# Norms between stages tile by tile, and act loads through GpSimd with one buffer less, in a 256-token model with expert retrieval

## The chip, the cores and the metric

One core of a Trainium2 chip runs the whole kernel. The time is that of one execution on the device in microseconds (us); lower is better. Engines: TensorE (PE) multiplies matrices, VectorE (DVE) and ScalarE (ACT) work on tiles of 128 partitions, GpSimd (POOL) and SyncE (SP) issue transfers (DMAs). Each engine runs its own list of instructions strictly in order and waits on semaphores for the others.

## The reference, cut to what matters

256 tokens of width 1024 pass through two blocks. The first block (attention, cross attention, feed-forward) ends in a norm. The second has two layers, each a mixer (an even and an odd kind) and an expert stage `peer`, with modulated norms ahead of both:

```python
x = _rmsnorm(x + (silu(gate) * up) @ w_down, final_norm)      # end of the first block
for l in range(2):
    h = rmsnorm(x, norm_mix[l]) * (1 + sc1) + sh1
    x = x + g1 * (even_mix(h) if l % 2 == 0 else odd_mix(h))
    h = rmsnorm(x, norm_ffn[l]) * (1 + sc2) + sh2
    x = x + g2 * peer(h, w_q[l], sub_keys[l], u[l], v[l])
return rmsnorm(x, final_norm_2)

def peer(h, w_q, sub_keys, u, v):            # per token t
    q = h @ w_q                              # 8 heads, two halves of 128
    top 16 of 128 x 128 keys by the scores of q against sub_keys, per head
    gate = softmax(the 16 scores)
    act = gelu(u[chosen] . h)
    return sum over heads and chosen of gate * act * v[chosen]
```

Everything is float32, and `u` and `v` have 16384 rows of 1024 each.

## The kernel before

Values of float32 are split into a high and a low half, and a product is three products on TensorE (high by high, high by low, low by high). Activations stand as `hl` tiles, channels on the partitions and the 256 tokens along the free axis; the tokens are two tiles `t` of 128. A weight comes as 1 MB `w` by a DMA that SyncE issues (`load_w`; in the V loop L1635); `split_w` makes its halves 512 columns at a time, the high one `wh` on ScalarE (L302), the low one `wl` on VectorE (L303). The ring `w` has three buffers, `wh`/`wl` five pairs.

The order of the stages: first block to about 366 us, where `w_down` ends (`proj`, with `ev_down` as what is done with its results); even_mix to 447; peer 0 to 1270; odd_mix to 1400; peer 1 to the end. Between two stages x is normed: `part_sq` (ScalarE, L154) sums squares of half a token tile, `inv_rms` makes 1/rms by a chain of some nine 128x1 instructions on VectorE (L181 to L199), `diag` (L212) puts it on a diagonal, and `to_T` (L267) multiplies x by the diagonal on TensorE, which transposes and scales it at once, 16 products of 128x128; `split_psum` (L249 to L255) adds the modulation and splits the result, pair of k by pair of k, into `hl`. While this goes on `keep_warm` (L287) lets TensorE run 80 products that nobody reads.

In `peer`, head by head, `feat2` multiplies h by `w_q` (L373 with the high half of the weight against 512 columns, L370 with the low half); its accumulators are two PSUM banks each, out of four banks in all (`acc_banks`, `acc_tile`). Then the top-16 search and the one-hot matrices `G` (gates of all experts, built from `onehots` and `build`) run beside the U stage, 64 passes of `feat2` over `u` that write `act` to DRAM in 256 KB pieces. The V loop follows, 64 passes: load 1 MB of `v`, split it (four `wh`, four `wl`), take 256 KB of `act` and of `G` for the same experts, and add 24 products of 512 columns to four accumulators (`wide_mm`, L423). `gated(n)` makes the activations for pass n: the load of `act` (SyncE, L1580) into `ag`, product by the gate `G` into `wt` (VectorE, L1582), its high half (ScalarE, L1589), its low half by subtraction (VectorE, L1590). `ag` and `wt` come from the ring `k2` with five buffers (NK2), as most temporaries do. In peer 0's V loop the modulation of the next layer is computed too, with an ada weight of 512 KB per pass (`ada_tick`; L482 loads it on SyncE, L483 multiplies on VectorE).

The order on each engine isn't written out: a scheduler walks through the program with estimated durations and queues instructions as they become ready, so it fixes each engine's list at build time; `follow` and `behind` give it hints.

Of the kernel before, what the change touches and what calls it, by code (L numbers as in the profile page):

```python
# [19 lines left out]
P = 128  # L20
S = 256
# [8 lines left out]
WARM = 80, 80, 80, 80  # L30
# [45 lines left out]
def body(tc, A, out, dbg=None, stop=None):  # L76
# [73 lines left out]
    def accum_sq(dst, src, eng):  # L150
        n = src.shape[-1]
        if eng == "a":
            j = st.tile([P, D], mybir.dt.bfloat16, name="k2", bufs=NK2)
            nc.scalar.activation(j[:, :n], src, AF.Square, accum_out=dst)  # L154
# [135 lines left out]

    def load_w(dram, off, per, ada=True):
# [6 lines left out]
    def split_w(src, n):  # L298

        h = sp.tile([P, 512], F32R, name="wh")  # L300
        l = sp.tile([P, 512], F32R, name="wl")
        ada_p["act"] = nc.scalar.activation(h[:, :n], src, AF.Copy).ins.name  # L302
        i_ = nc.vector.tensor_sub(l[:, :n], src, h[:, :n].bitcast(F32))  # L303
        ada_p["after"] = i_.ins.name
        return h, l
# [51 lines left out]
    def feat2(hl, dram, off, evac):  # L357
# [4 lines left out]
        for q in range(4):  # L362
            wh, wl = split_w(w[:, q * 512:(q + 1) * 512], 512)
            to = acc[:, q // 2]
            for i in range(4):
                k = (q % 2) * 4 + i
                ws = slice(i * P, (i + 1) * P)

                def low():
                    nc.tensor.matmul(to[:, 0, :], wl[:, ws], part(hl, k, 0), start=False, stop=False)  # L370
                if k == 7:
                    low()
                nc.tensor.matmul(to.rearrange("p a s -> p (a s)"), wh[:, ws],  # L373
                                 hl[k // 2][:, k % 2].rearrange("p a s -> p (a s)"), start=k == 0, stop=k == 7)
                if k < 7:
                    low()
            tick()
        evac(acc)

    def proj(hl, kc, dram, off, n, evac, base=0, quiet=0, turn=None):  # L380
# [10 lines left out]
        for k in order:  # L391
            m = min(4, kc - k)
            w = load_w(dram, off + k * P * n, m * n, len(order) - order.index(k) > quiet)
            j = 0
            while j < m:

                final = k == order[-1]
                js = [j, j + 1] if final and j == m - 2 else [j]
                if final and turn:
                    js = [turn[i] for i in js]  # L400
                ws = [split_w(w[:, q * n:(q + 1) * n], n) for q in js]
                last = None
                for t in range(2):
                    sl = slice(t * P, (t + 1) * P)
                    for q, (wh, wl) in zip(js, ws):
                        h_, l_ = pick(base + k + q, sl)
                        i_ = mm3(ps[t][:, :n], h_, l_, wh[:, :n], wl[:, :n], k == order[0] and j == 0 and q == js[0],
                                 final and j + len(js) == m and q == js[-1], after=last)
                        last = i_.ins.name if len(js) == 2 else None
                    if final and j + len(js) == m:  # L410
                        evac(t, ps[t][:, :n])
                for _ in js:
                    tick()
                j += len(js)
# [552 lines left out]

    def ev_down(hf):
        hs = slice(hf * 512, (hf + 1) * 512)

        def f(t, ps):
# [3 lines left out]
            part_sq(ssf, xf, t, hf, "a")  # L975
        return f
    ada_p["rate"] = RD
    for hf in range(2):
        proj(pick_g, 22, A["w_down"], hf * FF * 512, 512, ev_down(hf), quiet=hf)
# [3 lines left out]


    r1_ = nrm.tile([P, 2], F32, name="r1_", bufs=1)
    r2_ = nrm.tile([P, 4], F32, name="r2_", bufs=1)
    by0 = []
    for t in range(2):
        a_, b_ = ssx[:, 2 * t:2 * t + 1], ssx[:, 2 * t + 1:2 * t + 2]
        e_, c_ = r2_[:, 2 * t:2 * t + 1], r2_[:, 2 * t + 1:2 * t + 2]  # L990
        nc.vector.tensor_scalar(e_, a_, b_, D * EPS, op0=OP.add, op1=OP.add)
        nc.vector.tensor_scalar(e_, e_, EPS, None, op0=OP.mult)
        inv_rms(c_, ssf[:, 2 * t:2 * t + 1], ssf[:, 2 * t + 1:2 * t + 2], e_)
        by0.append(diag(c_))
    for t in range(2):
        inv_rms(r1_[:, t:t + 1], ssx[:, 2 * t:2 * t + 1], ssx[:, 2 * t + 1:2 * t + 2])
    if stop in ("mix", "cross", "b1"):
        for t in range(2):
# [17 lines left out]
    def x_scales(ss):  # L1016

        r = nrm.tile([P, 2], F32, name="rx2")
        out_ = []
        for t in range(2):  # L1020
            inv_rms(r[:, t:t + 1], ss[:, 2 * t:2 * t + 1], ss[:, 2 * t + 1:2 * t + 2])
            out_.append(diag(r[:, t:t + 1]))
        return out_
# [810 lines left out]
```

## Time and profile before

| | us |
|---|---|
| median of 3 runs | 2221.74 |
| lowest and highest | 2216.76, 2221.75 |
| profiled execution | 2223.68 |
| its span in the trace | 2221.9 |
| TensorE busy | 2183.6 (98%) |
| VectorE busy | 1826.7 (82%) |
| ScalarE busy | 1326.6 (60%) |
| GpSimd busy | 21.2 (1%) |

Busy shares are means over the span. The chain of work that ended last lies for 84% on TensorE, for 7% on VectorE and for 6% on the loads of `act`. By stretches: 40 slices of the page show TensorE at 9 tenths or more everywhere but at the two ends, and the DMA engines between 1 and 9 tenths, highest in peer 0's V loop (about 940 to 1270 us).

### The profile page before, as it was taken

The page shows a single profiled execution, that of the slowest core. Times are in us where ns is not written, and L with a number is a line of the kernel's source. Part 1 is how long each engine was busy: PE and PEld are TensorE (multiplying, and loading weights), DVE is VectorE, ACT ScalarE, POOL GpSimd, SP SyncE. Part 2 cuts the span into 40 slices and gives each one's busy share as a digit, 9 for nine tenths or more (in the row PEclk, how much of TensorE's full clock was granted, in tenths as well). Part 3 has the DMA queues.
Part 4 walks back from the last instruction along what each step waited for, and adds up shares of the span by engine and source line. Part 5 has one row for each costly group of instructions (what it writes and reads, how often), then busy time and mean ns, then how long its engine had stood idle before and what let it go on. Part 6 is the DMA issues. An engine that isn't in the chain of part 4 may idle for free.

```text
span 2221.9 us, 36167 instructions
## 1 busy us (share of the span) xinstructions
PE 2183.6 (98%) x12792; PEld 1865.7 (84%) x12792; DVE 1826.7 (82%) x4379; ACT 1326.6 (60%) x2448; POOL 21.2 (1%) x28
## 2 busy tenths in 40 slices
PE   8999999999999999999999999999999999999998
PEld 7889998888888888878777787888888888888886
DVE  7778888689988887688888888899888876777776
ACT  7656555555666666555555566566666666555554
POOL 0000000000000000000000010000000000000000
PEclk9999999999999999999999999999999999999999
DMA  6246787445655555889999643456555557666663
GB/s 244 96 167 256 271 303 281 160 173 206 226 212 207 198 212 209 283 314 332 323 321 322 215 157 122 171 193 239 203 201 210 196 212 259 250 248 245 244 240 143
DMA packets 107286, 503.30 MB, mean 227 GB/s; under 512 B 12513, under 2 KB 13665, under 8 KB 61794
## 3 DMA queue, kind: packets, MB, share of 16 engines
q1 hardware_dynamic: 87954, 465.19, 58.4%
q10 hardware_dynamic: 18864, 33.72, 4.1%
q8 instruction: 100, 1.64, 0.3%
q0 software_dynamic: 288, 2.10, 0.2%
q14 instruction: 80, 0.66, 0.1%
HBM read 464.25 MB, written 36.70 MB: 225 GB/s over the span
## 4 chain that ended last, share of the span: by engine, by line
PE 84%; DVE 7%; DMA 6%; ACT 1%; issue 1%; SPq 0%; DVEq 0%; ACTq 0%
PE acc L373 24%; PE acc L423 22%; PE acc L370 12%; DMA k<-act 6%; PE acc L308 4%; PE acc L311 4%; PE acc L312 4%; DVE wl L303 3%; PE acc L320 3%; PE acc L321 3%; PE acc L319 3%; PE mm L1547 1%; PE mm L1548 1%; DVE G L483 1%; PE pt L267 1%
## 5 line engine op out<-in xcount | busy, mean ns | idle before, releaser
L302 ACT ACTIVATE wh<-w 128x512 fp32r<-128x512 f32 (+1 forms) x1408 | 879.6, 630 | 652.6 <-PE acc L423 247.5
L303 DVE TENSOR_TENSOR wl<-w,wh 128x512 fp32r<-128x512 f32 (+1 forms) x1408 | 951.9, 689 | 205.7 <-ACT wh L302 198.2
L373 PE MATMUL acc<-q,wh 128*128 128x512 f32 x2240 | 797.3, 402 | 0.0
L423 PE MATMUL acc<-wh,q 128*128 128x512 f32 x1984 | 611.0, 390 | 0.0
L370 PE MATMUL acc<-q,wl 128*128 128x256 f32 x2240 | 584.3, 281 | 1.0 <-DVE wl L303 1.0
L373 PEld LDWEIGHTS acc<-q,wh 128*128 128x128 f32 x2240 | 408.1, 188 | 69.9
L370 PEld LDWEIGHTS acc<-q,wl 128*128 128x128 f32 x2240 | 422.6, 189 | 22.7 <-DVE wl L303 2.1
L423 PEld LDWEIGHTS acc<-wh,q 128*128 128x128 f32 x1984 | 372.4, 188 | 76.7
L423 PE MATMUL acc<-wl,q 128*128 128x512 f32 x992 | 387.4, 392 | 7.3 <-DVE wl L303 7.0
L423 PEld LDWEIGHTS acc<-wl,q 128*128 128x128 f32 x992 | 186.2, 188 | 52.7 <-DVE wl L303 14.5
L1582 DVE SCALAR_TENSOR_TENSOR k<-k,G 128x512 f32<-128x512 f32 x128 | 88.2, 690 | 65.9 <-DMA k<-act 65.0
L1410 ACT ACTIVATE k<-acc 128x512 f32<-128x512 f32 x124 | 74.0, 597 | 96.9 <-PE acc L373 96.8
L320 PE MATMUL acc<-q,wh 128*128 128x256 f32 x416 | 117.8, 284 | 0.5 <-DVE q L245 0.5
L319 PE MATMUL acc<-q,wh 128*128 128x256 f32 x416 | 117.3, 283 | 0.7 <-ACT q L244 0.7
L321 PE MATMUL acc<-q,wl 128*128 128x256 f32 x416 | 117.5, 283 | 0.0
L1411 DVE TENSOR_TENSOR k<-acc,k 128x512 f32<-128x512 f32 x124 | 85.0, 686 | 17.6 <-ACT k L1410 17.3
L311 PE MATMUL acc<-wl,q 128*128 128x512 f32 (+1 forms) x224 | 89.4, 400 | 0.0
L1590 DVE TENSOR_TENSOR q<-k,q 128x512 fp32r<-128x512 f32 x126 | 86.2, 684 | 0.8
L312 PE MATMUL acc<-wh,q 128*128 128x512 f32 (+1 forms) x224 | 86.6, 400 | 0.0
L308 PE MATMUL acc<-wh,q 128*128 128x512 f32 (+1 forms) x224 | 85.9, 402 | 0.4 <-ACT q L244 0.4
L1589 ACT ACTIVATE q<-k 128x512 fp32r<-128x512 f32 x126 | 77.8, 617 | 13.8 <-DVE k L1582 13.8
L320 PEld LDWEIGHTS acc<-q,wh 128*128 128x128 f32 x416 | 79.7, 192 | 0.8 <-DVE q L245 0.7
(459 smaller groups left out, 2660.4 us busy)
## 6 DMA issues: line engine op xcount, KB each, us to landing
w<-in_peer_u_dram SPq DMA_DIRECT2D x128, 1024.0 KB, 4.9
w<-in_peer_v_dram SPq DMA_DIRECT2D x128, 1024.0 KB, 5.3
act<-k ACTq DMA_DIRECT2D x128, 256.0 KB, 3.0
k<-act SPq DMA_DIRECT2D x128, 256.0 KB, 5.4
G<-in_ada_w_dram SPq DMA_DIRECT2D x52, 512.0 KB, 7.2
w<-in_w_gu_dram SPq DMA_DIRECT2D x22, 1024.0 KB, 4.8
adw<-in_ada_w_dram SPq DMA_DIRECT2D x44, 512.0 KB, 5.6
w<-in_peer_w_q_dram SPq DMA_DIRECT2D x16, 1024.0 KB, 4.9
```

The source lines that it names most:

```text
L302: ada_p["act"] = nc.scalar.activation(h[:, :n], src, AF.Copy).ins.name
L303: i_ = nc.vector.tensor_sub(l[:, :n], src, h[:, :n].bitcast(F32))
L308: i_ = nc.tensor.matmul(ps, lh, wh, start=start, stop=False)
L311: nc.tensor.matmul(ps, lh, wl, start=False, stop=False)
L312: i_ = nc.tensor.matmul(ps, ll, wh, start=False, stop=stop)
L319: nc.tensor.matmul(ps, wh, h, start=start, stop=False)
L320: nc.tensor.matmul(ps, wh, l, start=False, stop=False)
L321: nc.tensor.matmul(ps, wl, h, start=False, stop=stop)
L370: nc.tensor.matmul(to[:, 0, :], wl[:, ws], part(hl, k, 0), start=False, stop=False)
L373: nc.tensor.matmul(to.rearrange("p a s -> p (a s)"), wh[:, ws], hl[k // 2][:, k % 2].rearrange("p a s -> p (a s)"), start=k == 0, stop=k == 7)
L423: nc.tensor.matmul(ps[t, hf], lhs, ww[hf], start=first and lhs is h and ww is wh, stop=last and lhs is l)
L1582: nc.vector.scalar_tensor_tensor(wt, ag, 1.0 / GATE, G[0][:, 2 * n:2 * n + 2, :], op0=OP.mult, op1=OP.mult)
```

## The change

It has seven parts.

1. `keep_warm` at each of the four transitions runs 48 products instead of 80.
2. `proj` takes `tail`: for the second half of `w_down` and of even_mix's output weight the last four k's (not two) are kept, and all their products for token tile 0 run ahead of all for tile 1. What follows a finished tile is now its norm too (`x1_scale`, `x_scale` in the callbacks), so the norm of tile 0 comes ahead of that of tile 1. `diag` takes a k2 buffer.
3. `mod_hT` writes out the 16 transposing products: all 8 of tile 0, then all 8 of tile 1, into two `pt` tiles and two accumulator tiles; a pair of k's is split after tile 1's product of it.
4. `norm_done` marks the norm as issued; of the next five weight splits the last four are ordered behind the norm's last square (ScalarE) and diagonal (VectorE).
5. For head 0 of each peer stage `feat2` takes the weight's quarters in the order 0 and 2, 1 and 3, both channels of a pair at once.
6. In `gated` the load of `act` is issued by GpSimd (L1623), and `wt` is `ag`: the product by the gate (L1625) writes into the loaded buffer. The onehots ring has three buffers instead of two, and the builds come two at a time.
7. The last norm and the four stores of the output move into peer 1's callbacks, tile by tile.

The core of the diff:

```diff
-WARM = 80, 80, 80, 80
+WARM = 48, 48, 48, 48
...
     def diag(r):
-        d = st.tile([P, P], F32, name="dg", bufs=2)
-        nc.vector.tensor_scalar(d, ident, r, None, op0=OP.mult)
+        d = st.tile([P, 512], F32, name="k2", bufs=NK2)[:, 0:P]
+        norm["diag"] = nc.vector.tensor_scalar(d, ident, r, None, op0=OP.mult).ins.name
         return d
+
+    def norm_done():
+        norm["act"], norm["dve"], norm["left"] = norm["last"], norm["diag"], 5
...
+        if norm["left"]:
+            norm["left"] -= 1
+            if norm["left"] < 4:
+                follow(a_, norm["act"])
+                follow(i_, norm["dve"])
         return h, l
...
-    def feat2(hl, dram, off, evac):
+    def feat2(hl, dram, off, evac, by_chunk=False):
...
+        for ps in [(0, 2), (1, 3)] if by_chunk else [(0,), (1,), (2,), (3,)]:
+            ws = [split_w(w[:, p_ * 512:(p_ + 1) * 512], 512) for p_ in ps]
             for i in range(4):
...
+                for p_, wp_ in zip(ps, ws):
+                    chunk(p_ // 2, p_ % 2 * 4 + i, *wp_)
...
+        tail = min(tail, kc)
+        for ks in [[k] for k in seq[:kc - tail]] + [seq[kc - tail:]]:
...
+            for t in range(2):
...
+                for k, (wh, wl) in zip(ks, ws):
+                    h_, l_ = pick(base + k, sl)
+                    i_ = mm3(ps[t][:, :n], h_, l_, wh[:, :n], wl[:, :n], k == seq[0], k == seq[-1], after=last)
...
+                if final:
+                    evac(t, ps[t][:, :n])
...
             part_sq(ssf, xf, t, hf, "a")
+            if hf:
+                x1_scale(t)
...
+        proj(pick_g, 22, A["w_down"], hf * FF * 512, 512, ev_down(hf), quiet=hf, tail=4 if hf else 2)
+    norm_done()
+    keep_warm(WARM[0])
...
         hl = hl_tiles(8)
-        to_T(lambda t, k: x[:, t, k * P:(k + 1) * P], 8, hl, gain=lambda k: a[:, k:k + 1], bias=lambda k: b[:, k:k + 1], by=by)
+
+        pts = [ptr.tile([P, 2, S], F32, name="pt") for _ in range(2)] + [acc_tile([P, 2, S]) for _ in range(2)]
+        for t in range(2):
+            for k in range(0, 8, 2):
+                for i in range(2):
+                    nc.tensor.matmul(pts[k // 2][:, i, t * P:(t + 1) * P], x[:, t, (k + i) * P:(k + i + 1) * P], by[t], start=True, stop=True)
+                if t:
+                    split_psum(hl, k, pts[k // 2], lambda k: a[:, k:k + 1], lambda k: b[:, k:k + 1])
...
-            e = ip.tile([P, 4, P], F16, name="ohe", bufs=2)
+            e = ip.tile([P, 4, P], F16, name="ohe", bufs=3)
...
             ag = st.tile([P, 2, S], F32, name="k2", bufs=NK2)
-            nc.sync.dma_start(ag.rearrange("p j t -> p (j t)"), actd[n])
-            wt = st.tile([P, 2, S], F32, name="k2", bufs=NK2)
+
+            nc.gpsimd.dma_start(ag.rearrange("p j t -> p (j t)"), actd[n])
+            wt = ag
             nc.vector.scalar_tensor_tensor(wt, ag, 1.0 / GATE, G[0][:, 2 * n:2 * n + 2, :], op0=OP.mult, op1=OP.mult)
...
+            def end(t):
+                if l == 0:
+                    by.append(x_scale(ss, t))
+                    return
...
+                    nc.sync.dma_start(out[t * P:(t + 1) * P, hs], xn[:, t, hs])
```

The lists of instructions that the scheduler makes of both kernels, at three places. In them a name is a buffer and its number, an arrow leads from the inputs to the output, and line numbers are those of the kernel in question.

VectorE in the middle of peer 1's V loop, before: `k2_22738` is the product of pass 21, `q4_22544` the low half (by subtraction) of pass 17.

```order
L303 TENSOR_TENSOR wl_22356<-w_22342,wh_22355 128x512
L303 TENSOR_TENSOR wl_22372<-w_22342,wh_22371 128x512
L303 TENSOR_TENSOR wl_22376<-w_22342,wh_22375 128x512
L303 TENSOR_TENSOR wl_22401<-w_22391,wh_22400 128x512
L1590 TENSOR_TENSOR q4_22495<-k2_22493,q4_22495 128x512
L303 TENSOR_TENSOR wl_22405<-w_22391,wh_22404 128x512
L1582 SCALAR_TENSOR_TENSOR k2_22689<-k2_22687,G_18092 128x512
L303 TENSOR_TENSOR wl_22421<-w_22391,wh_22420 128x512
L303 TENSOR_TENSOR wl_22425<-w_22391,wh_22424 128x512
L303 TENSOR_TENSOR wl_22450<-w_22440,wh_22449 128x512
L1590 TENSOR_TENSOR q4_22544<-k2_22542,q4_22544 128x512
L1582 SCALAR_TENSOR_TENSOR k2_22738<-k2_22736,G_18092 128x512
```

The same place in the changed kernel (L308 is the low half of a weight, L1625 the product, L1633 the subtraction): `k2_22526` is pass 21, `q4_22289` and `q4_22337` are passes 16 and 17.

```order
L308 TENSOR_TENSOR wl_22173<-w_22140,wh_22172 128x512
L1625 SCALAR_TENSOR_TENSOR k2_22478<-k2_22478,G_17903 128x512
L308 TENSOR_TENSOR wl_22197<-w_22188,wh_22196 128x512
L1633 TENSOR_TENSOR q4_22289<-k2_22286,q4_22289 128x512
L308 TENSOR_TENSOR wl_22201<-w_22188,wh_22200 128x512
L308 TENSOR_TENSOR wl_22217<-w_22188,wh_22216 128x512
L1625 SCALAR_TENSOR_TENSOR k2_22526<-k2_22526,G_17903 128x512
L308 TENSOR_TENSOR wl_22221<-w_22188,wh_22220 128x512
L308 TENSOR_TENSOR wl_22245<-w_22236,wh_22244 128x512
L1633 TENSOR_TENSOR q4_22337<-k2_22334,q4_22337 128x512
L308 TENSOR_TENSOR wl_22249<-w_22236,wh_22248 128x512
```

The product of pass 21 stood behind the subtraction of pass 17 and now stands ahead of it, with two low halves in between; it reads and writes the buffer that the subtraction of pass 16 frees.

VectorE in peer 0's V loop, changed kernel: `q4_12526` is written by the subtraction of a pass four ahead of that of `k2_12723`, the product two rows below it.

```order
L1625 SCALAR_TENSOR_TENSOR k2_12673<-k2_12673,G_7419 128x512
L308 TENSOR_TENSOR wl_12383<-w_12370,wh_12382 128x512
L308 TENSOR_TENSOR wl_12399<-w_12370,wh_12398 128x512
L308 TENSOR_TENSOR wl_12403<-w_12370,wh_12402 128x512
L506 SCALAR_TENSOR_TENSOR G_7419,mod_86<-G_7419 128x1024
L308 TENSOR_TENSOR wl_12430<-w_12421,wh_12429 128x512
L1633 TENSOR_TENSOR q4_12526<-k2_12523,q4_12526 128x512
L511 TENSOR_TENSOR mod_86<-mod_86,cols_81 128x8
L1625 SCALAR_TENSOR_TENSOR k2_12723<-k2_12723,G_7419 128x512
L308 TENSOR_TENSOR wl_12434<-w_12421,wh_12433 128x512
L308 TENSOR_TENSOR wl_12450<-w_12421,wh_12449 128x512
```

Here the subtraction stayed ahead of the product, as it is before the change in both loops, with low halves and an ada product (L506) between one product and the next subtraction.

TensorE at the start of peer 0, before: `pt` are the tiles into which x is transposed, `acc_5474` and `acc_5528` the scores of heads 0 and 1.

```order
L267 MATMUL pt_5413<-dg_5361,xf_2111 128x128
L267 MATMUL pt_5413<-dg_5373,xf_2111 128x128
L267 MATMUL pt_5413<-dg_5361,xf_2111 128x128
L267 MATMUL pt_5413<-dg_5373,xf_2111 128x128
L373 MATMUL acc_5474<-q4_5383,wh_5475 128x512
L370 MATMUL acc_5474<-q4_5383,wl_5476 128x256
L373 MATMUL acc_5528<-q4_5383,wh_5529 128x512
L370 MATMUL acc_5528<-q4_5383,wl_5530 128x256
L267 MATMUL pt_5426<-dg_5361,xf_2111 128x128
L267 MATMUL pt_5426<-dg_5373,xf_2111 128x128
L267 MATMUL pt_5426<-dg_5361,xf_2111 128x128
L267 MATMUL pt_5426<-dg_5373,xf_2111 128x128
```

The same place in the changed kernel, where `acc_5326` and `acc_5327` are accumulator tiles that take transposes and `acc_5411` is head 0:

```order
L1062 MATMUL acc_5326<-k2_5231,xf_2111 128x128 x2
L1062 MATMUL acc_5327<-k2_5231,xf_2111 128x128 x2
L1062 MATMUL pt_5324<-k2_5261,xf_2111 128x128 x2
L1062 MATMUL pt_5325<-k2_5261,xf_2111 128x128 x2
L1062 MATMUL acc_5326<-k2_5261,xf_2111 128x128 x2
L1062 MATMUL acc_5327<-k2_5261,xf_2111 128x128 x2
L383 MATMUL acc_5411<-q4_5320,wh_5412 128x512
L380 MATMUL acc_5411<-q4_5320,wl_5413 128x256
L383 MATMUL acc_5411<-q4_5320,wh_5416 128x512
L380 MATMUL acc_5411<-q4_5320,wl_5417 128x256
L383 MATMUL acc_5411<-q4_5320,wh_5412 128x512
```

All 16 transposes now stand ahead of the first real product, those of tile 0 (diagonal `k2_5231`) first; head 1 no longer runs beside head 0, and head 0's accumulators come out of the same four banks as the two transposed tiles.

## Rows read from the trace of the kernel before

**Rows 1.** The page: busy us, share of the span and instructions of each engine.

```profile
PE 2183.6 (98%) x12792; PEld 1865.7 (84%) x12792; DVE 1826.7 (82%) x4379; ACT 1326.6 (60%) x2448; POOL 21.2 (1%) x28
```

**Rows 2.** Busy time by window: V loops of peer 0 and peer 1.

```profile
core 0: us, PE busy (x) PEld busy (x) DVE busy (x) ACT busy (x) POOL busy (x), PEclk, DMA share, GB/s
...
945.00:1265.00 320.00, 312.73 (x1365) 253.19 (x1364) 272.58 (x486) 177.04 (x291) 0.00 (x0) 1.00 0.86 309
...
1895.00:2205.00 310.00, 310.00 (x1373) 256.78 (x1372) 223.28 (x347) 172.04 (x283) 0.00 (x0) 1.00 0.66 237
```

**Rows 3.** VectorE in order of time, peer 1's V loop: start, duration, instruction.

```profile
2020.91 0.68 DVE L1590 TENSOR_TENSOR q<-k,q 128x512 fp32r<-128x512 f32 x1
2021.66 0.69 DVE L303 TENSOR_TENSOR wl<-w,wh 128x512 fp32r<-128x512 f32 x1
2022.27 0.68 DVE L1582 SCALAR_TENSOR_TENSOR k<-k,G 128x512 f32<-128x512 f32 x1
```

**Rows 4.** SyncE's issues in order of time, the same stretch.

```profile
2022.98 0.32 SPq L1580 DMA_DIRECT2D k<-act  x1
```

**Rows 5.** The loads of act (L1580), 1900 to 2200 us: who waited, landing.

```profile
  DVE k L1582: 12.6, 10
...
DMA to landing us min/median/max: 2.4/3.2/6.2
```

**Rows 6.** The loads of v (L1635), 1900 to 2200 us: first and last start, landing.

```profile
L1635 SPq DMA_DIRECT2D w<-in_peer_v_dram x54: 327/333/333, 1900.0 to 2189.3; - x54
...
DMA to landing us min/median/max: 4.6/4.7/7.2
```

**Rows 7.** DMA issues: source, engine, count, size, median us from issue to landing.

```profile
xd<-xf POOLq DMA_DIRECT2D x1, 1024.0 KB, 5.7
xd<-x POOLq DMA_DIRECT2D x1, 1024.0 KB, 6.9
```

**Rows 8.** The loads of act (L1580), 950 to 1200 us: starts, who waited, landing.

```profile
L1580 SPq DMA_DIRECT2D k<-act x46: 319/327/436, 954.9 to 1199.8; - x46
...
  DVE k L1582: 35.4, 35
...
DMA to landing us min/median/max: 4.7/6.5/8.3
```

**Rows 9.** TensorE's waits, 945 to 1265 us: total, times, longest.

```profile
PE acc L423 <- DVE wl L303: 7.0, 11, 1.1
```

**Rows 10.** All engines in order of time, from w_down's end into even_mix.

```profile
366.56 4.64 PE L287 MATMUL mm<-iota 128*128 128x128 f16 x80
...
372.95 2.02 PE L267 MATMUL pt<-dg,xf 128*128 128x128 f32 x16 [1.75 <-DVE r__4483 L193]
373.00 0.28 DVE L212 TENSOR_SCALAR dg<-ck,r__4483 128x128 f32<-128x128 f32 x1
...
374.94 0.48 DVE L254 SCALAR_TENSOR_TENSOR k<-pt,a,q 128x256 f32<-128x256 f32 x1 [1.59 <-ACT q L253]
```

**Rows 11.** The same view, from even_mix into peer 0.

```profile
452.14 2.19 PE L267 MATMUL pt<-dg,xf 128*128 128x128 f32 x16 [0.32 <-DVE dg L212]
...
454.29 0.48 DVE L254 SCALAR_TENSOR_TENSOR k<-pt,a,q 128x256 f32<-128x256 f32 x1 [1.62 <-ACT q L253]
454.69 0.54 DVE L249 TENSOR_SCALAR k<-pt,a,mod 128x256 f32<-128x256 f32 x1
...
455.38 1.13 PE L267 MATMUL pt<-dg,xf 128*128 128x128 f32 x8 [1.05 <-DVE k L249]
...
456.26 0.47 PE L373 MATMUL acc<-q,wh 128*128 128x512 f32 x1
```

**Rows 12.** TensorE in order of time, from peer 0 into odd_mix.

```profile
1276.18 0.71 PE L267 MATMUL pt<-dg,x 128*128 128x128 f32 x4 [1.28 <-DVE dg L212]
```

**Rows 13.** TensorE in order of time, from odd_mix into peer 1.

```profile
1405.98 2.35 PE L267 MATMUL pt<-dg,x 128*128 128x128 f32 x16 [1.34 <-DVE rs_v L186]
```

**Rows 14.** Busy time by window, a stretch of even_mix (columns as in rows 2).

```profile
420.00:425.00 5.00, 5.00 (x19) 3.74 (x19) 1.32 (x4) 1.53 (x4) 0.00 (x0) 0.76 0.00 0
```

More of the change, by code (lines that the diff above doesn't have):

```diff
@@ L153, in accum_sq @@
             j = st.tile([P, D], mybir.dt.bfloat16, name="k2", bufs=NK2)
-            nc.scalar.activation(j[:, :n], src, AF.Square, accum_out=dst)
+            norm["last"] = nc.scalar.activation(j[:, :n], src, AF.Square, accum_out=dst).ins.name
         else:
@@ L289, in keep_warm @@
             name = i_.ins.name
+    norm = {"left": 0}
     def load_w(dram, off, per, ada=True):
@@ L390, in proj @@
         order = list(range(0, kc, 4))
[L391 to L414, printed above, removed]
+        pieces = {}
@@ new lines, in piece @@
+        def piece(k):
+            g = k - k % 4
+            if g not in pieces:
+                m = min(4, kc - g)
+                pieces[g] = load_w(dram, off + g * P * n, m * n, len(order) - order.index(g) > quiet)
+            return pieces[g], k % 4
+        seq = list(range(kc))
+        if turn:
+            seq[-4:] = [seq[-4:][i] for i in turn]
+        tail = min(tail, kc)
+        for ks in [[k] for k in seq[:kc - tail]] + [seq[kc - tail:]]:
+            ws = []
+            for k in ks:
+                w, q = piece(k)
+                ws.append(split_w(w[:, q * n:(q + 1) * n], n))
+            final = ks[-1] == seq[-1]
+            last = None
+            for t in range(2):
+                sl = slice(t * P, (t + 1) * P)
+                for k, (wh, wl) in zip(ks, ws):
+                    h_, l_ = pick(base + k, sl)
+                    i_ = mm3(ps[t][:, :n], h_, l_, wh[:, :n], wl[:, :n], k == seq[0], k == seq[-1], after=last)
+                    last = i_.ins.name if len(ks) > 1 else None
+                if final:
+                    evac(t, ps[t][:, :n])
+            for _ in ks:
+                tick()
@@ L978, in body @@
     for hf in range(2):
-        proj(pick_g, 22, A["w_down"], hf * FF * 512, 512, ev_down(hf), quiet=hf)
+        proj(pick_g, 22, A["w_down"], hf * FF * 512, 512, ev_down(hf), quiet=hf, tail=4 if hf else 2)
+    norm_done()
     keep_warm(WARM[0])
     ff.close()
[L985 to L996, printed above, removed]
     if stop in ("mix", "cross", "b1"):
+        x1_rms()
         for t in range(2):
@@ L1014, in ab_cols, with x_scale @@
         return a, mod[:, l, base:base + 8]
[L1016 to L1023, printed above, removed]
+    def x_scale(ss, t):
+        r = nrm.tile([P, 1], F32, name="rx1", bufs=2)
+        inv_rms(r, ss[:, 2 * t:2 * t + 1], ss[:, 2 * t + 1:2 * t + 2])
+        return diag(r)
     def mod_hT(l, which, x, by, stack):
@@ L1065, in even_mix @@
         hl = mod_hT(0, "mix", x, by, s0)
+        x1_rms()
         for t in range(2):
@@ L1348, in odd_mix @@
         ss = nrm.tile([P, 4], F32, name="ssx", bufs=1)
-        ga = gated_add(x, grow, ew, ss)
+        by = []
+        ga = gated_add(x, grow, ew, ss, by)
         for h in range(4, 8):
@@ L1564, in peer @@
         for h in range(8):
-            feat2(hl, A["peer_w_q_2"], (l * 8 + h) * P * 2048, scores(h))
+            feat2(hl, A["peer_w_q_2"], (l * 8 + h) * P * 2048, scores(h), by_chunk=h == 0)
         side.popleft()[1]()
@@ L1676, in body @@
         return
-    x, ss, xs_ = peer(0, x, by, b1)
+    x, by, xs_ = peer(0, x, by, b1)
     dump("xp0", x)
@@ L1681, in body @@
         return
-    by = odd_mix(x, x_scales(ss))
+    by = odd_mix(x, by)
     dump("xm1", x)
@@ L1686, in body @@
         return
-    x, ss, xs_, frow = peer(1, x, by, xs_)
-    r_ = nrm.tile([P, 2], F32, name="rx2")
-    o = out.rearrange("(t p) d -> p t d", p=P)
-    for t in range(2):
-        inv_rms(r_[:, t:t + 1], ss[:, 2 * t:2 * t + 1], ss[:, 2 * t + 1:2 * t + 2])
-        for hf in range(2):
-            hs = slice(hf * 512, (hf + 1) * 512)
-            nc.vector.scalar_tensor_tensor(x[:, t, hs], x[:, t, hs], r_[:, t:t + 1], frow[:, hs], op0=OP.mult, op1=OP.mult)
-            nc.sync.dma_start(o[:, t, hs], x[:, t, hs])
+    x, by, xs_ = peer(1, x, by, xs_)
     xs_.close()
```

81 lines of the change are left out of this document (53 added, 28 removed).

## The prediction

> **What bounds the kernel now.** Read the page's busy line first: TensorE is busy for 2183.6 of 2221.9 us [rows 1], so a change can give back at most the 38 us in which TensorE does nothing, plus the filler products at the four transitions between stages (80 each, 4.64 us [rows 10]). It can cost without limit, wherever another engine becomes slower than TensorE. Next, the windows of the two V loops (the 64 passes at the end of each peer stage): in peer 0's TensorE is busy for 312.73 of 320 us, in peer 1's for 310.00 of 310 [rows 2]. The waits behind this: in peer 0's loop TensorE waited 11 times, 7.0 us in all, each time for a low half written by VectorE [rows 9]; in peer 1's loop there is no TensorE wait at all. One pass of peer 1's loop takes (2189.3 − 1900.0)/53 = 5.46 us, counted on its weight loads [rows 6]; peer 0's takes (1199.8 − 954.9)/45 = 5.44 us, on its act loads [rows 8]. What the changed kernel must keep below 5.46 us is therefore every other cycle of that loop.
>
> **Act loads on GpSimd, one buffer for two, peer 1.** This part carries the forecast. Before, a pass took two buffers of the k2 ring of 5 (load `ag`, product `wt`), and the load of `ag` was issued when an earlier product L1582 had read its buffer: product at 2022.27, 0.68 long, issue at 2022.98, that is 0.03 after its end [rows 3, 4]. In between that product and the one that needs the data stand three or four low halves and one subtraction; the loads land in 2.4 to 6.2 us, median 3.2, and the product waited for them only 10 times in 300 us, 12.6 us [rows 5], at no cost to TensorE.
>
> Now product and load share the buffer, and a pass takes one. With 5 buffers the load of pass n waits for the last reader of pass n−5's, and that is the subtraction (L1633), no longer the product. The order pieces show what VectorE does meanwhile. In peer 1 it has the product of pass n *ahead of* the subtraction of pass n−4: after the subtraction of n−5 come two or three low halves, then the product of n, then one or two low halves, then the subtraction of n−4. VectorE works strictly in this order, so a loop closes: subtraction ends, GpSimd issues the load (0.03), the load lands (call that L), the product runs (0.61, the step from one 512-wide instruction to the next, 2021.66 to 2022.27 [rows 3]), one low half (0.61), the subtraction (0.68), and the next load may go. The pass is L + 1.93 us. Behind the waiting load on GpSimd stands only the next load; behind the waiting product on VectorE stand the low halves of the weights, which TensorE needs. In 53 of the 64 passes the product stands ahead of the subtraction like that: 38 with one low half between, 13 with two (L + 2.54), 2 with none (L + 1.32); the mean is L + 2.06. TensorE's 5.46 is the longer one as long as L is at most 3.40 us; above that every 0.1 us of L costs 5.3 us. What hid the landing before, almost a whole pass, is gone.
>
> L is not shown by this trace: no 256 KB load was issued by GpSimd. From below, it cannot beat what SyncE's loads need there, 2.4 at least and 3.2 in the median [rows 5]: passes of 4.5 and 5.3, no loss. Nearest are the two transfers that GpSimd did issue, `xd` with 1 MB each, 5.7 and 6.9 us [rows 7]. On SyncE's queue 1 MB weights land in 4.6 us at best and 256 KB in 2.4 [rows 5, 6], so the smaller size takes off 2.2: 3.5 and 4.7 us. Both `xd` ran beside a few weight loads, while in the V loop the DMA engines are busy 66% of the time [rows 2]; SyncE's own median there is 0.8 above its best [rows 5], which put on 4.7 gives 5.5 at most. I take 4.2, just above the middle of 3.5 and 4.7, as these are the only rows of that queue. The pass is then 6.26, and the loss (6.26 − 5.46) × 53 = **+42 us**. At 3.5 it is (5.56 − 5.46) × 53 = +5; at 4.7, +69; at 5.0, +85; at 5.5, +111.
>
> The Trainium skill, "DMA: Bandwidth & Descriptors", section "Anatomy of one DMA — SWDGE (gpsimd) path", fits such a transfer as 2.0 us plus the bytes over 436 kB per us; by it 256 KB would be 2.6 us, an estimate, and the loop 4.7 us, so no loss at all. The same formula makes 4.4 us of `xd`'s 1 MB, where the rows have 5.7 and 6.9; the rows decide, and what would follow from 2.6 us is the first rival below.
>
> **The same in peer 0.** Here the order pieces show the subtraction of n−4 ahead of the product of n. The loop then spans two passes: load (L), product 0.61, three low halves 1.83, one 1024-wide instruction on an ada weight (about 1.2, twice a low half), another low half 0.61, the subtraction 0.68: L + 4.97 for 2 × 5.44, so L may be 5.9. Before, SyncE's loads took 4.7 to 8.3 there, median 6.5, as they stand behind a 1 MB weight and a 512 KB ada load in one queue, and the product waited 35.4 us for them [rows 8]; this is what makes the low halves late. On a queue of its own the load escapes the line. It must still share the engines, at 86% busy [rows 2]: 4.2 plus some 1 us, under 5.9. TensorE's 7.0 us can go, and I take −4; bounds −7 and, with L of 7 in the crowd, (5.99 − 5.44) × 46 = +25. SyncE's queue loses these issues in both loops, which makes no weight later.
>
> **The four ends.** The most to be had: 80 filler products become 48, 4.64 × 32/80 = 1.86 us off each, and the gaps behind them go: 1.75 at the first, 0.32 and 1.05 at the second, 1.28 at the third, 1.34 at the fourth [rows 10 to 13]. That is 7.4 + 5.7 = 13.2 us. Against it: the filler is followed by a wait for VectorE at each end, so shortening the filler alone gives nothing; only an earlier norm does.
> - End 1 (after w_down, tail 4 instead of 2): the first token tile finishes 12 products before the second instead of 6, so its norm starts 6 × 0.23 = 1.4 us earlier, and so do the first transposes. But behind the second tile's diagonal VectorE now has four low halves (2.4 us), a 1024-wide scale and four products of wsT, roughly 4 us, ahead of the first low half of h that TensorE needs. Before that half stood 1.9 us behind its diagonal (373.00 to 374.94 [rows 10]). I take +0.6; bounds −1.9 and +2.
> - Ends 2 and 4 (into a peer stage): half of the 16 transposes now write two accumulator tiles, and head 0's scores need those same PSUM banks. So its first real product waits until VectorE and ScalarE have split all of k = 4 to 7; before, real products were mixed in after the split of the first pair, at 456.26 [rows 11], and of two heads at once. A pair of k's is three VectorE instructions of some 0.40 (454.29 to 454.69 [rows 11]), so three more pairs are 3.6 us. This eats the earlier norm: +0.5 each, bounds −3 and +3.
> - End 3 (into odd_mix): products wait for single pairs as before, the first transposes come earlier: −2, bounds −3.5 and 0.
> - The last end: the second tile's chain stays the last one: 0.
> Sum of ends: +0.6 + 0.5 + 0.5 − 2 = about 0; bounds −12 and +8.
>
> The held-back splits at these ends (four of the next weights' pairs behind the norm) are work that comes anyway; their cost is in the VectorE queue at end 1. Loading onehots in three buffers and building in pairs moves work within the U stage, where TensorE is the bound: 0.
>
> **Sum.** 2223.7 (the profiled run) + 42 − 4 + 0 = 2261.7. The profiled run is 1.9 above the median of the runs, so **2260 us**.
>
> **Rivals.**
> - *The loop doesn't close.* L is 3.4 or less, as on SyncE's queue (median 3.2). Then peer 1 stays at 5.46, peer 0 gains 4 to 7, the ends up to 5: 2221.7 − 9 = 2213. For it: SyncE's median [rows 5]. Against it: both rows of GpSimd's queue [rows 7]. It decides at 3.4 us. Chance 0.18. The formula of the Trainium skill's page quoted above points here.
> - *Just at the edge*: L from 3.4 to 3.65, a loss of 0 to 13 against gains of 4 to 9: within 6.7 us of before, about 2220. Chance 0.12. (6.7 us is 0.3%, about what a measurement here tells from no change.)
> - *A crowded queue*: L of 5 or more, because packets of the load share each DMA engine with the weight that is under way: +85 and more in peer 1, perhaps +25 in peer 0: 2305 or more. For it: 66% and 86% DMA share. Chance 0.10.
> - *The clock.* The granted clock fell to 0.76 in one stretch of before, 420 to 425, where TensorE ran 19 products in 5 us [rows 14]: a mean of the full level, 2.4 GHz, and the lower one, 1.2. With 48 filler products TensorE may idle longer at the ends and find the lower level. At half speed for 3 us this costs 1.5 per end, 6 in all; the sign of the forecast stays, so it is inside the range.
>
> **How the numbers follow.** L between 3.65 and 5 has 0.60 (2224 to 2300, middle 2260); with the crowded queue slower has 0.70, same 0.12, faster 0.18. The range leaves out one in ten on either side: the better half of the first rival below 2210, the crowded queue above 2302.
>
> **What would show it.** In the after profile: peer 1's weight loads 6.0 to 6.7 us apart instead of 5.46; L1623's landings near 4.2 us; VectorE's product L1625 waiting for the load in nearly every pass, and TensorE idle behind low halves (L308) there, some 40 us. In peer 0's loop TensorE's waits fall under 4 us. If landings are under 3.4, the forecast's sign is wrong; if they are above and peer 1 still runs at 5.46, the loop is. First real products at the ends: within 2 us of before.

## The result, and the profile after

The changed kernel takes 2246.47 us (median of 4 runs, 2243.69 to 2248.83) against 2221.74 before: 1.0113 times as long, 95% interval 1.009 to 1.0135. The profiled execution spans 2244.9 us, 23.0 more than before. The forecast was slower, 2260, range 2210 to 2302.

Cut into stretches (from the start of one transition's filler products to the next, and within a peer stage at the first and the last weight load of a V-loop product on TensorE), both traces say where the 23 us are:

| stretch | before | after | forecast | measured |
|---|---|---|---|---|
| start to the first transition | 366.6 | 365.7 | 0 | −0.9 |
| even_mix with its start (end 1) | 80.6 | 80.5 | +0.6 | −0.1 |
| peer 0 up to the V loop (end 2) | 460.2 | 463.6 | +0.5 | +3.4 |
| peer 0, V loop | 356.9 | 353.6 | −4 | −3.3 |
| from there to odd_mix | 6.0 | 6.3 | 0 | +0.3 |
| odd_mix with its start (end 3) | 129.8 | 129.4 | −2 | −0.4 |
| peer 1 up to the V loop (end 4) | 461.5 | 463.5 | +0.5 | +2.0 |
| peer 1, V loop | 343.8 | 365.4 | +42 | **+21.6** |
| last end | 16.6 | 16.9 | 0 | +0.3 |

Nearly all of it is peer 1's V loop. TensorE's waits in it, none before, are these (who waits for whom: us in total, times, longest):

```profile
PE acc L446 <- DVE wl L308: 11.5, 16, 3.5
PE acc L446 <- ACT q L1632: 1.5, 1, 1.5
```

They sum to 13.0 of the 21.6 us. The rest are stalls too short to be listed: a product's record lasts 0.39 us while the next product starts 0.23 us later. Counted from start to start, 59 steps of more than 0.24 us add 21.3 us to this loop; before, 6 such steps add 0.5. The granted clock, 0.88 in 2100 to 2105 us and 0.78 in 2105 to 2110 around the longest wait, explains at most (0.12 + 0.22) × 5 = 1.7 us of it.

VectorE in order of time shows the cause. L1633 is the subtraction, L1625 the product, L308 a low half of a weight:

```profile
2040.71 0.68 DVE L1633 TENSOR_TENSOR q<-k,q 128x512 fp32r<-128x512 f32 x1
2041.32 1.89 DVE L308 TENSOR_TENSOR wl<-w,wh 128x512 fp32r<-128x512 f32 x3
2045.74 0.69 DVE L1625 SCALAR_TENSOR_TENSOR k<-k,G 128x512 f32<-128x512 f32 x1 [2.53 <-DMA k<-act]
2046.35 0.68 DVE L308 TENSOR_TENSOR wl<-w,wh 128x512 fp32r<-128x512 f32 x1
2046.95 0.68 DVE L1633 TENSOR_TENSOR q<-k,q 128x512 fp32r<-128x512 f32 x1
2047.55 1.89 DVE L308 TENSOR_TENSOR wl<-w,wh 128x512 fp32r<-128x512 f32 x3
2051.12 0.69 DVE L1625 SCALAR_TENSOR_TENSOR k<-k,G 128x512 f32<-128x512 f32 x1 [1.68 <-DMA k<-act]
2051.73 0.69 DVE L308 TENSOR_TENSOR wl<-w,wh 128x512 fp32r<-128x512 f32 x1
2052.33 0.68 DVE L1633 TENSOR_TENSOR q<-k,q 128x512 fp32r<-128x512 f32 x1
```

and GpSimd's issues beside it:

```profile
2041.69 0.55 POOL L1623 DMA_DIRECT2D k<-act  x1 [5.25 <-DVE q L1633]
2047.93 0.55 POOL L1623 DMA_DIRECT2D k<-act  x1 [5.69 <-DVE q L1633]
2053.31 0.55 POOL L1623 DMA_DIRECT2D k<-act  x1 [4.84 <-DVE q L1633]
```

Read as a circle: the subtraction ends at 2041.39, GpSimd issues at 2041.69, the product can start at 2045.74, one low half, the subtraction of 2046.95 ends at 2047.63, the next issue is at 2047.93. Before, around the product of [rows 3], VectorE sat idle only behind ScalarE's high halves of the weights:

```profile
2020.30 0.69 DVE L303 TENSOR_TENSOR wl<-w,wh 128x512 fp32r<-128x512 f32 x1 [0.67 <-ACT wh L302]
```

The loads of act by line, 1870 to 2240 us (who waited; time to landing), answer to [rows 5], and the weight loads, 1900 to 2220 us, to [rows 6]:

```profile
  DVE k L1625: 114.9, 55
...
DMA to landing us min/median/max: 2.7/3.0/7.5
```

```profile
L1678 SPq DMA_DIRECT2D w<-in_peer_v_dram x55: 327/328/328, 1901.4 to 2211.7; - x55
```

In the window of [rows 5], 1900 to 2200 us, the product waited 50 times, 107.6 us, where it had waited 10 times, 12.6. A pass takes (2211.7 − 1901.4)/54 = 5.75 us on the mean of this window, 5.46 before.

The starts of the peer stages show the second loss. TensorE, from even_mix into peer 0 (answers to [rows 11]), then the windows around it:

```profile
446.19 2.85 PE L290 MATMUL mm<-iota 128*128 128x128 f16 x48
...
451.76 1.06 PE L1062 MATMUL acc<-k,xf 128*128 128x128 f32 x8
457.31 0.77 PE L383 MATMUL acc<-q,wh 128*128 128x512 f32 x1 [4.49 <-DVE k L252]
```

```profile
447.00:457.00 10.00, 5.82 (x69) 5.52 (x66) 9.65 (x33) 7.80 (x17) 0.69 (x1) 0.91 0.55 211
457.00:462.00 5.00, 4.69 (x15) 4.05 (x16) 1.07 (x5) 0.46 (x2) 0.00 (x0) 0.50 0.58 210
```

The transposes are done at 452.8, yet head 0 starts at 457.31, and then runs at the lower clock (0.50, 1.2 GHz) until 462.

### The profile page after: what moved, and what is told of

The parts are those of the page before. It is cut to its first block, busy times and chain, and to the rows that moved or that the text cites. A ratio compares the mean times of both kernels' runs of the same rounds, so it can differ in the third digit from the quotient of the medians.

```text
span 2244.9 us, 36022 instructions
## 1 busy us (share of the span) xinstructions
PE 2186.4 (97%) x12664; PEld 1863.5 (83%) x12664; DVE 1810.8 (81%) x4379; ACT 1327.1 (59%) x2448; POOL 91.0 (4%) x156
## 4 chain that ended last, share of the span: by engine, by line
PE 65%; issue 25%; DVE 4%; POOL 3%; DMA 2%; ACT 1%; SPq 0%; POOLq 0%; DVEq 0%; ACTq 0%
PE acc L383 23%; PE acc L380 12%; PE acc L446 4%; PE acc L320 4%; PE acc L324 4%; PE acc L323 4%; POOL k L1623 3%; PE acc L332 3%; PE acc L333 3%; PE acc L331 3%; PE mm L1587 1%; PE mm L1588 1%; DVE wl L308 1%; DMA k<-act 1%; PE mm L1462 1%
## 5 line engine op out<-in xcount | busy, mean ns | idle before, releaser
L308 DVE TENSOR_TENSOR wl<-w,wh 128x512 fp32r<-128x512 f32 (+1 forms) x1408 | 943.1, 689 | 179.0 <-ACT wh L307 173.6
L383 PEld LDWEIGHTS acc<-q,wh 128*128 128x128 f32 x2240 | 408.0, 189 | 82.6 <-issue 9.9
L380 PEld LDWEIGHTS acc<-q,wl 128*128 128x128 f32 x2240 | 424.5, 190 | 24.7 <-DVE wl L308 2.5
L1625 DVE SCALAR_TENSOR_TENSOR k<-k,G 128x512 f32<-128x512 f32 x128 | 88.5, 691 | 161.4 <-DMA k<-act 161.2
L1623 POOL DMA_DIRECT2D k<-act x128 | 70.0, 547 | 1494.1 <-PE acc L383 866.2
L1633 DVE TENSOR_TENSOR q<-k,q 128x512 fp32r<-128x512 f32 x126 | 86.4, 686 | 0.1
```

The costliest lines, as they stand in the source:

```text
L1623: nc.gpsimd.dma_start(ag.rearrange("p j t -> p (j t)"), actd[n])
```

## The experiments

Times are compared with runs of the kernel before on the same chip. Behind each ratio stands its 95% interval. Lengths of V loops and of starts are from the profiled execution of each.

**The order alone.** The changed kernel, with the product held behind the subtraction of four passes before.

```diff
-            nc.vector.scalar_tensor_tensor(wt, ag, 1.0 / GATE, G[0][:, 2 * n:2 * n + 2, :], op0=OP.mult, op1=OP.mult)
+            i_ = nc.vector.scalar_tensor_tensor(wt, ag, 1.0 / GATE, G[0][:, 2 * n:2 * n + 2, :], op0=OP.mult, op1=OP.mult)
+            if n > 4:
+                follow(i_, subs[n - 4])
...
-            nc.vector.tensor_sub(wl_, wt, wh_.bitcast(F32))
+            subs.append(nc.vector.tensor_sub(wl_, wt, wh_.bitcast(F32)).ins.name)
```

> The changed kernel with one thing added: in the V loops the product of pass n is ordered behind the subtraction of pass n-4 on VectorE. Same buffers, same GpSimd queue. Theory of the closed loop (subtraction of n-5, load, product of n, subtraction of n-4, all within one pass): with the order turned the loop spans two passes, peer 1's weight loads go back from 5.75 to 5.46 us apart, TensorE's waits there vanish, about -20 us: 2226 (2223 to 2231). Rival, the GpSimd queue itself (its transfers slow the weights or land too late in any order): still 5.7 us a pass, 2246.

Measured: 2224.03 us, ratio 1.0004 (0.9993 to 1.0015). Peer 1's V loop is 345.3 us instead of 365.4, and TensorE has no wait in it from 1960 to 2170 us. The loads of act by line, 1960 to 2170 us (who waited: us, times; time to landing):

```profile
  DVE k L1627: 1.0, 3
...
DMA to landing us min/median/max: 3.0/3.6/5.3
```

They land no sooner (median 3.6), but only 3 products wait, 1.0 us in all. Queue, buffers and bytes are the same; the order of two instructions on VectorE is worth 20 us. The closed loop stands.

**The queue.** The changed kernel with the loads back on SyncE.

```diff
-            nc.gpsimd.dma_start(ag.rearrange("p j t -> p (j t)"), actd[n])
+            nc.sync.dma_start(ag.rearrange("p j t -> p (j t)"), actd[n])
```

> The changed kernel with the loads of act issued by SyncE again, the shared buffer kept. The order in peer 1 still has the product of n ahead of the subtraction of n-4 (26 passes with one low half between, 26 with two). Theory of the closed loop: the pass is 0.03 + L + 0.61 + 0.9 + 0.68 = L + 2.2 on SyncE's queue too; L is 2.4 at best and more behind a 1 MB weight, so 5.5 to 6.2 us a pass, 2225 to 2265, and the product waits for its load in nearly every pass. Rival, the GpSimd queue is what costs: back to 5.46 a pass with no waits, 2222 to 2226.

Measured: 2244.63, ratio 1.0099 (1.0075 to 1.0124). Peer 1's V loop 365.4, the same as with GpSimd, and the product waits in every pass (the same view, 1960 to 2170 us):

```profile
  DVE k L1625: 77.7, 36
...
DMA to landing us min/median/max: 2.5/3.4/5.7
```

The GpSimd queue isn't what costs.

**The shared buffer alone**, in the kernel before.

```diff
-            wt = st.tile([P, 2, S], F32, name="k2", bufs=NK2)
+            wt = ag
```

> The kernel before with the shared buffer alone (the product writes into the loaded buffer), loads on SyncE, ends as before. Theory of the closed loop: same order as in the previous run, so peer 1 gets 5.5 to 6.2 us a pass and the kernel is slower than before by 2 to 40 us: 2224 to 2262. Rival, queue or ends: 2222, 5.46 a pass.

Measured: 2241.31, ratio 1.0083 (1.0059 to 1.0106). Peer 1's V loop 363.1 (+19.3), peer 0's 350.5 (−6.4). This one line carries the loss in peer 1; and peer 0's gain is there without GpSimd.

**Transposes pair by pair again**, the rest as changed; no accumulator tiles.

```diff
-        pts = [ptr.tile([P, 2, S], F32, name="pt") for _ in range(2)] + [acc_tile([P, 2, S]) for _ in range(2)]
-        for t in range(2):
...
+        to_T(lambda t, k: x[:, t, k * P:(k + 1) * P], 8, hl, gain=lambda k: a[:, k:k + 1], bias=lambda k: b[:, k:k + 1], by=by)
```

> The changed kernel with the transposes of mod_hT written as before: pair of k by pair of k, both token tiles, into the two pt tiles only. Theory of the bank wait (head 0 waits for the accumulators that hold half of the transposes): at both starts of a peer stage the 4.4 us gap ahead of head 0 shrinks to 1 us or so and the granted clock stays at 1.0 there; -4 to -7 us: 2241. Rival, the gap comes from the splits that VectorE holds back: gap unchanged, 2246.

Measured: 2240.97, ratio 1.0088 (1.0064 to 1.0111). This interval overlaps that of the changed kernel (1.009 to 1.0135), and the profiled execution was the fastest of the four, 2232.46, by a short V loop of peer 0 (347.4); so the lengths of the starts decide, not the time. The starts of the peer stages take 459.7 and 460.3 us instead of 463.6 and 463.5. TensorE in order of time at the first:

```profile
446.48 2.85 PE L290 MATMUL mm<-iota 128*128 128x128 f16 x48
...
454.39 1.13 PE L270 MATMUL pt<-k,xf 128*128 128x128 f32 x8 [1.74 <-DVE k L252]
455.28 0.47 PE L383 MATMUL acc<-q,wh 128*128 128x512 f32 x1
```

Head 0 starts 8.8 us behind the filler's start, with 11.1 in the changed kernel and 9.1 before, and the granted clock is 1.00 from 447 to 462 us, though the four low halves that the rival blamed still stand ahead of the splits. So the banks, with the lower clock that followed the wait, were the loss there: 3.9 and 3.2 us. What is left of the change there (norm by tiles, 48 filler products) is ahead of before by 0.5 and 1.2 us.

**Both cures together**: the edits of the first and the fourth experiment.

> The changed kernel with both cures: transposes pair by pair as before, and the product of n ordered behind the subtraction of n-4. Theory (loop and bank wait are the two costs, they add): peer 1's V loop at 345 us as with the order alone, both stretches from the transition to the V loop at 460 instead of 463.6: 2224 - 4 - 4 = 2216 (2211 to 2220), faster than the kernel before by 0.1 to 0.5%. Rival, the gains do not add because a faster end only makes TensorE wait later for VectorE: 2220 to 2224.

Measured: 2220.61, ratio 0.9988 (0.9979 to 0.9997). Where the gains were expected they came, 345.3 us for peer 1's V loop and 459.8 and 460.3 for the starts, but the time is 4.6 us above the forecast's middle and lies in the rival's range, 2220 to 2224. Even_mix took 84.0 us in its profiled execution, 80.5 in the changed kernel. The granted clock fell twice there, to 0.80 in 375 to 380 us, behind gaps of 2.23 and 2.44 us of TensorE, and to 0.83 in 420 to 430, where the kernel before had its stretch too [rows 14]. That this is what made even_mix longer isn't shown: the kernel of the fourth experiment has the same lists there and a fall of its own (0.74 in 370 to 375), and took 80.9.

**The same with 80 filler products** (`WARM` as before).

> The kernel of the previous run with 80 filler products at each transition instead of 48. Theory (the norm behind the filler sets the end, the filler only fills): within 2 us of the previous run, 2214 to 2218; first real products at most 1 us later, granted clock 1.0 behind every transition. Rival, the clock: where 48 products left the granted clock at 0.91 over the 20 us behind the first transition, 80 keep it at 1.0 and each such place gains up to 1.5 us: 2212 to 2215.

Measured: 2218.54, ratio 0.9984 (0.9974 to 0.9994), 0.5 above the forecast. Even_mix 80.9 us, and the granted clock is 1.00 in every window from 365 to 452 us. The two intervals overlap: that 80 are better than 48 isn't settled by the times; the two traces with 48 and transposes by pairs are the ones with the lower clock there.

**The shared buffer with the order, in the kernel before**: the edits of the third and the first experiment.

> The kernel before with the shared buffer and the order of product behind subtraction; loads on SyncE, ends as before. Theory (sharing gives peer 0 its gain, the order keeps peer 1 open): peer 0's V loop 350 to 353 instead of 357, peer 1's 344 to 346: 2222 - 5 + 1 = 2218 (2214 to 2221). Rival, the gain in peer 0 came from fewer waits in SyncE's queue, which needs GpSimd: 357 as before, 2222.

Measured: 2220.11, ratio 0.9988 (0.9978 to 0.9997). Peer 1's V loop 344.1, as forecast; peer 0's 353.1, in a profiled execution that was the longest of twelve (2224.94).

**GpSimd alone, in the kernel before**: two buffers per pass as there.

```diff
-            nc.sync.dma_start(ag.rearrange("p j t -> p (j t)"), actd[n])
+            nc.gpsimd.dma_start(ag.rearrange("p j t -> p (j t)"), actd[n])
```

> The kernel before with nothing but the loads of act issued by GpSimd; two buffers per pass as before, so a load waits for the product of the pass ahead. Loop theory: in peer 1 the loop product, load, product is 0.68 + 0.37 + 3.5 = 4.6 us, under 5.46, so peer 1's V loop stays at 344; in peer 0 the scheduler now puts the product of n right ahead of the subtraction of n, so a late load delays what TensorE needs at once: 357 to 370. In all 2220 to 2236. Rival, the GpSimd queue costs by itself: peer 1's V loop also grows, by 10 us or more.

Measured: 2213.61, ratio 0.9955 (0.994 to 0.9971): faster than every kernel so far, where no gain had been expected. Peer 1's V loop 345.6 as the loop theory said; peer 0's is 345.5 instead of 356.9. TensorE's waits from 945 to 1265 us (total, times, longest), against [rows 9]:

```profile
PE pt L267 <- DVE dg L212: 1.9, 2, 1.5
```

These are at the transition; within the loop not one of the 11 waits is left, and no product waits for a load. The expected harm of having the product of n right ahead of its own subtraction didn't come. The loads, with a queue of their own, land in 3.5 to 6.9 us, median 5.2, where SyncE's needed 6.5 [rows 8]. But VectorE's order in peer 0's loop changed with the queue: a subtraction follows a product after two low halves, where three low halves and the ada product stood between. How much of the gain is the queue's and how much the order's wasn't tried apart.

**The changed kernel with the one line undone** (a buffer of its own for the product, GpSimd kept).

> The whole changed kernel with one line undone: the product writes into a buffer of its own again (two buffers per pass); loads stay on GpSimd. Theory (the shared buffer is the whole cost, GpSimd is a gain in peer 0): peer 1's V loop 346, peer 0's 346, the starts of the peer stages still 463.6 each: 2213.6 of the run with GpSimd alone plus 3.4 + 2 = 2219 (2216 to 2222). Rival, other parts of the change cost in the V loops too: 2225 or more.

Measured: 2219.75, ratio 0.9988 (0.9979 to 0.9997). V loops 345.4 and 345.6, starts of the peer stages 463.1 and 464.6. Without the shared buffer the change is 0.1% faster than before; its ends keep back 6 of the 9 us that GpSimd alone gains.

**Everything cured**: GpSimd, two buffers, transposes pair by pair, 80 filler products, norms by tiles.

> Loads on GpSimd with two buffers, transposes pair by pair, 80 filler products, and the rest of the change (norm tile by tile, held-back splits). Theory (every cost found is cured, the ends then bring up to 1 us each): 2210 to 2213, at or a little under the run with GpSimd alone (2213.6) and faster than both kernels. Rival, the norm by tiles brings nothing once the transposes go by pairs: 2213 to 2216.

Measured: 2213.55, ratio 0.9962 (0.995 to 0.9974), the same as GpSimd alone: the rival. V loops 345.5 and 345.6, starts 459.8 and 460.4, even_mix 80.9. Its window over peer 0's loop, against [rows 2] (the last 12 us lie behind the loop):

```profile
945.00:1265.00 320.00, 319.65 (x1480) 265.43 (x1478) 284.29 (x514) 177.18 (x303) 28.49 (x53) 1.00 0.88 314
```

**Both edits of the V loop alone**, without the ends.

> The kernel before with both edits of the V loop (loads on GpSimd and the shared buffer) and none of the ends. Theory: the loop as in the changed kernel, peer 1's V loop 365, peer 0's 351 to 354, and the ends as before: 2222 + 21 - 4 = 2239 (2235 to 2243); what the other parts cost in the changed kernel is the rest, 5 us or so at the starts of the peer stages. Rival, the ends are free: 2246.

Measured: 2243.4, ratio 1.0084 (1.0068 to 1.0099), 0.4 above the forecast. By the medians the ends cost the changed kernel 3.1 us, by the differences to before (24.7 and 20.6) 4.1; the intervals don't tell this from the 5 that were expected. V loops 350.4 and 367.3, starts 460.2 and 461.5 as before.

## Why the prediction was right, and where it wasn't

**The mechanism in peer 1 was right.** The product ahead of the subtraction closes a loop within one pass, and it decides the sign. Five kernels with the loop closed (the changed one, SyncE, the shared buffer alone, transposes by pairs, both edits of the V loop) have peer 1's V loop at 363 to 367 us, whichever queue loads and whatever the ends; the seven without it, by order or by a second buffer, have 344 to 346. The clock isn't the cause: with SyncE it doesn't fall in that loop, which is as long.

**Its size was twice too large**, 42 for 21.6 us. Taken pass by pass from 1960 to 2170 us (35 passes in the order of time of VectorE and GpSimd), the terms are:

| term | forecast | measured, mean |
|---|---|---|
| end of the subtraction to the issue | 0.03 | 0.37 (median 0.30) |
| issue to the start of the product (L) | 4.2 | 3.51 (median 3.10, up to 5.50) |
| product, low halves, subtraction | 2.03 | 2.05 |
| pass | 6.26 | 5.93 |

(The passes of this stretch are longer than those of the whole loop, 5.75.) L is the mis-sized term. It was taken from two 1 MB transfers of the trace of before, 5.7 and 6.9 us [rows 7], less 2.2 for the size. In the trace after, the same two read

```profile
xd<-xf POOLq DMA_DIRECT2D x1, 1024.0 KB, 4.3
xd<-x POOLq DMA_DIRECT2D x1, 1024.0 KB, 4.3
```

and the packets in the traces say why. Before, 1.0 MB of SyncE's queue was moving when each `xd` was issued, until 2.9 and 4.1 us later, and `xd`'s own packets started 2.3 and 2.5 us behind the issue. After, no packet of SyncE's queue was under way, and they started after 1.3 and 1.1 us. (Without such packets it can still take longer: the second one took 5.5 us in the run with the order alone.) So the rows of before held some 2 us of other traffic, and a value close to the better one, 3.5, would have been right. The loads of `act` show the same: of the 52 from 1890 to 2190 us, 15 landed in 3.8 us or more; in 14 of these the load's own packets started 2.4 to 2.9 us behind the issue, with 1.0 MB or more of SyncE's queue beside them, and in the quicker ones after 1.3 to 1.5. The Trainium skill, "DMA: Bandwidth & Descriptors", section "Anatomy of one DMA — SWDGE (gpsimd) path", fits a transfer on this path as 2.0 us plus the bytes over 436 kB per us; an estimate by it is 2.6 us for 256 KB and 4.4 for 1 MB. The trace agrees for transfers that meet little else: the least landing here was 2.7, and `xd` took 4.3. By it alone the loop would have cost nothing. The issue delay was a row read across queues: 0.03 us is SyncE's, GpSimd's is ten times that.

**Part of the sign was luck.** With the measured mean of L, 3.51, and the forecast's other terms the loss would have come out as (3.51 + 2.06 − 5.46) × 53 = 6 us, and the forecast as no change. The issue delay that it lacked, 0.34 us a pass, is worth 0.34 × 53 = 18 us. So L was 0.7 too long and the issue 0.34 too short, and the two errors made up for each other in part. The signs that it named came smaller too: weight loads 5.75 us apart and not 6.0 to 6.7, TensorE's recorded waits 13 us and not 40.

**The first rival's point was wrong in kind.** It was to decide at a landing of 3.4 us, and the median landing was 3.0, under it. Yet the kernel is slower: the loop adds every pass's own L, so the mean with its tail up to 5.50 counts, and behind it another 0.34 for the issue. Measured, the loop breaks even at 5.46 − 0.37 − 2.05 = 3.04 us of mean L. So a threshold on the median would have called the sign wrongly; the forecast had it right because it took 4.2.

**Peer 0's loop** gave −3.3 for −4, but the reason given, a queue of its own, isn't what the runs show. With the shared buffer and the loads on SyncE the loop takes 352.2 us (the changed kernel with SyncE) and 350.5 (the shared buffer alone), no more than with GpSimd, and the loads land in 6.6 and 6.4 us in the median, as late as before [rows 8]. Why the shared buffer shortens this loop stays open. By the prediction's sum the loop over two passes allows 5.9 us of L, and GpSimd's landings had a median of 6.0 there (2.9 to 7.3), so it stood on its own edge. With two buffers GpSimd's queue gives 11.4 us (345.5), more than the bound of −7, which had been set by TensorE's recorded waits. Those leave out the short stalls: counted from start to start, 44 steps of more than 0.24 us add 12.3 us to this loop before, and 7 such steps 2.2 us with GpSimd alone, which is 10.1 of the 11.4.

**Ends 2 and 4** were forecast at +0.5 each and cost 3.4 and 2.0, the first a little over its bound of +3. The bank wait was there as described. VectorE in order of time at the first of them, the last diagonal before:

```profile
452.38 0.28 DVE L212 TENSOR_SCALAR dg<-ck,rx 128x128 f32<-128x128 f32 x1
```

and after:

```profile
450.42 0.29 DVE L212 TENSOR_SCALAR k<-ck,rx 128x128 f32<-128x128 f32 x1
450.62 2.49 DVE L308 TENSOR_TENSOR wl<-w,wh 128x512 fp32r<-128x512 f32 x4
453.03 0.48 DVE L257 SCALAR_TENSOR_TENSOR k<-pt,a,q 128x256 f32<-128x256 f32 x1
...
456.63 0.54 DVE L252 TENSOR_SCALAR k<-acc,a,mod 128x256 f32<-128x256 f32 x1
```

Counted from the filler's start, the last diagonal stands at 4.2 us where it stood at 5.2, so the norm is 1 us earlier. But four held-back low halves come first, and the splits of all pairs, from 453.03 to 457.17, begin at 6.8 where they began at 7.1. The prediction had put the cost of these low halves at end 1 alone. Head 0 then starts 4.3 us behind the first split, where it was 2.0 [rows 11]. That makes 11.1 us from the filler's start instead of 9.1, and 11.6 instead of 10.3 at the second one: 2.0 and 1.3 us of the loss. The rest came behind head 0's start, and there the prediction had no term for the clock: after those 4.49 us without work the granted clock was 0.50 from 457 to 462, and 0.66 in 1410 to 1415 at the second one, after 4.43 us. The clock rival had looked for this behind the shorter filler; it came behind the gap.

**End 3** gave −0.4 for −2. The pair of traces isn't enough for that: odd_mix with its start took 129.8 to 133.5 us in the five kernels with the ends of before, and 127.8 to 129.8 in the eight with the new ones, which is nearer to −2. **End 1** gave −0.1 for +0.6: there the first real product came earlier (7.9 us behind the filler's start, where it was 8.4), and TensorE then waited behind the work that the prediction named (four low halves, the scale, wsT):

```profile
377.15 0.74 PE L324 MATMUL acc<-wh,q 128*128 128x512 f32 x2 [2.41 <-ACT q L258]
```

**What stays open.** Peer 0's V loop varied between executions whose lists are alike in it: 347.4 (transposes by pairs), 353.6 (the changed kernel). Differences of up to 6 us in that loop between the runs with the shared buffer may be that; the three kernels with GpSimd and two buffers have 345.4 to 345.5. With either queue peer 1's pass comes to nearly the same (5.93 by GpSimd; 0.03 + 3.61 + 2.20 = 5.84 by SyncE): what SyncE issues sooner comes back as a longer L behind the weight loads in its queue and as more low halves between; that this is more than chance wasn't tried.

## To carry to other kernels

When two uses of a buffer are merged, look for who now frees it and what stands between that reader and the next one on the same engine: if the next load's consumer is queued ahead of the reader that frees the buffer after that, the transfer's whole latency is in the loop. Such a loop is paid by the mean of the latency and not by its median, and the cure can be an order of two instructions or one buffer, not another queue. A queue of its own for a small load that waits behind large ones, with the order that the scheduler then made, gained 9 us here, and the whole change lost 25; try the parts of a change apart.

## What the hardware showed

GpSimd issued a load 0.30 us (median) behind the VectorE instruction that released it, SyncE 0.03. GpSimd's 256 KB loads landed in 2.7 us at best and 7.5 at worst beside a stream of 1 MB weights in peer 1's loop, later where more of the other queue's bytes were under way. TensorE without work for 4.49 us was followed by half clock (0.50 in 457 to 462 us). And TensorE's recorded waits understated what was to be had: 7.0 us in peer 0's loop, while the long steps from start to start add 12.3, and the kernel with GpSimd alone is 11.4 faster there.
